# Attention over 64 heads: score buffers in one PSUM tile, and the order of all engines read from a table

## The chip, the cores and the metric

The kernel runs on one core of a Trainium2 chip. A core has five engines that run side by side, each with its own queue of instructions: TensorE (PE; its weight loads are shown as PEld) multiplies matrices into PSUM, VectorE (DVE) and ScalarE (ACT) work on PSUM and SBUF, GpSimd (POOL) on SBUF, and SyncE (SP) issues most DMA transfers. Instructions of different engines wait for each other by semaphores. The metric is the device time in microseconds of one execution. The median of three runs of the kernel before is 113.97 us (113.85 to 114.29).

## The reference

```python
batch, heads, seq, dim = 8, 8, 512, 64
...
scale = 1.0 / np.sqrt(q.shape[-1])
scores = np.einsum('bhqd,bhkd->bhqk', q, k) * scale
scores = scores - scores.max(axis=-1, keepdims=True)
attn = np.exp(scores)
attn = attn / attn.sum(axis=-1, keepdims=True)
return np.einsum('bhqk,bhkd->bhqd', attn, v).astype(np.float32)
```

There are 64 independent heads. Each has 512 x 512 scores; their exponentials, 16.8 million in all, weight the rows of v. Inputs and the output are float32, 8.4 MB each.

## The kernel before

**Tiling.** Heads are taken in 32 pairs; the two heads of a pair, called a and b here (h = 0, 1), share loads. A head's keys are cut into four blocks c of 128. One block of scores is 128 keys x 512 queries. Two blocks make a group, 1024 columns of 128 partitions, and a group is what one exponential works on. There are 128 groups; the last is done in two halves, so m runs from 0 to 128. In most pairs a group joins the same block of heads a and b, whose score matmuls use the two halves of TensorE's rows at the same time; in the first and the last pair a group joins two blocks of one head.

**The steps of a pair.** SyncE loads q, k and v of the pair, 256 KB each, into seven buffers per input. GpSimd casts each to float16 (`cast`, L515 for v, L525 for k and q). TensorE transposes k and q, four transposes each (`transposes`, L558), into one of two PSUM banks, and VectorE copies the result to SBUF (`copy`, L571). TensorE makes the scores of a group with two matmuls (`scores`, L598) in a PSUM buffer `st`, of which there are three. ScalarE writes the exponentials as float16 in `pt` (L602); 24 such buffers are there. Sixteen groups, listed in `ON_DVE`, go to VectorE instead: `raise_` (L625) makes the bits of a power of two from the scores, and five passes over SBUF (`pass_`: L642 and L651 take mantissa and exponent, L659, L661 and L665 a polynomial) correct it; the result is two tiles, `pe` and `pd`, so these blocks need two matmuls each where others need one.

**Values and output.** For 128 queries of a head, a unit, TensorE multiplies the four blocks' exponentials with v, to which a column of ones is joined (`values`, L704): 65 columns, the last being the sum of the weights. Seven units share a PSUM bank, one of the two that the transposes use too. VectorE takes reciprocals of the sums (`reciprocal`, L671) and multiplies (`normalise`, L676) into a ring of 112 units, from which SyncE stores heads, singly or in pairs. The last head has its own path (`last_values`, `finish`), with the last two groups' halves.

**The order.** All instructions are written out in the order that a planner, class `Plan`, finds: it steps through time in 5 ns with fixed costs for each instruction and decides for every engine what comes next. `ON_DVE`, due times of the casts and other numbers were set by hand in it. `cast_behind` ties each cast to an earlier instruction of VectorE (the number `behind` counts back along VectorE's instructions), so that GpSimd's casts lie beside chosen work of VectorE. A few exponentials (`KNOWN`) are tied to the cast six before.

**Buffers of scores.** `st` is a tile of a pool with three buffers, so a score pair waits until the reader of the group three before is done:

```python
st = ps_st.tile([P, 2, S], FP32, tag="st", name=f"st_{m}")
...
nc.tensor.matmul(st[:, x, cols], kc, qc[:, cols], start=True, stop=True)
```

**The start.** Pair 0 has its own code (`first_pair`): 52 small matmuls into a score buffer ahead of the data, casts split over three engines, and exponentials of its first group in two halves (L801).

Of the kernel before, what the change touches and what calls it, by code (L numbers as in the profile page):

```python
# [17 lines left out]
class Plan:  # L18

    SLOT, EXP, EXP_DONE, EXP_FIXED = 216, 853, 181, 64  # L20
    INTO, OUT_OF = 96, 96
    TRANSPOSE, V_UNIT = 222, 128
    TO_ACT, TO_DVE, TO_PE = 220, 210, 60

    COPY, NORM, RAISE = (601, 690), (50, 133), (1132, 1215)
    RECIPROCAL = 115
    SCALE, PRODUCT, EXTRA = 333, 600, 29
    COPY_1 = (400, 190)
    NORM_COLUMN, PASS_DONE = 67, 115
    PASSES = (SCALE, SCALE, PRODUCT, SCALE, PRODUCT)  # L30
    BITS = 2
    NEEDS = (None, None, 0, 2, 3)
    FIRST_EXP = 5000
    STEP = 5
    CALM, KEEN = 9000, 4
    FIRST_UNIT = 4
    KNOWN, OVER = (13, 15, 18, 20, 22, 24, 27, 42, 50, 61, 69, 97), 6
    ON_DVE = (5, 10, 16, 25, 28, 39, 44, 54, 63, 66, 74, 81, 91, 96, 103, 116)

    LATE_NORM, LATE_COPY, HURRY, SOON, BACKLOG = 700, 1500, 800, 160, 600  # L40
    LATE_MUL, WAIT = 400, 200
    SLACK, AHEAD = 0, 2

    CAST, CAST_PORT, CAST_DONE, TO_POOL = 557, 475, 130, 150
    SCALE_PORT, PRODUCT_PORT, GAP, REACH = 271, 537, 20, 5
    FIRST_LAND, LOAD, STORE, LATENCY, ISSUE = 5200, 752, 376, 2300, 470
    QUEUED, URGENT = 3500, 16
    PAIRED, STORE_ISSUE = 18, 520
    RAW, QK16, NV, NU = 7, 5, 12, 112
    PAIR, DUEK, DUEV, DUEL, PRE = 3300, 3550, 6000, 5000, 0  # L50

    def __init__(self, groups, pairs, first):
        self.groups, self.pairs = groups, pairs
        self.pe, self.act, self.dve = 7000, self.FIRST_EXP, 6300
        self.pool, self.port, self.dma = 4600, 4600, self.FIRST_LAND
        self.m, self.tiled = first, True
        self.read = []
        self.exps = {}
        for m in range(first):
            self.act += self.EXP + self.EXP_FIXED  # L60
            self.exps[m] = self.act + self.EXP_DONE
            self.read.append(self.exps[m])
        self.tq = {0: 5800}
        self.transposed = {0: 5800}
        self.next_t = 1
        self.part_t = 0
        self.banks = [5100, 5800]
        self.todo = [(g, h) for g in range(pairs) for h in range(2)]
        self.last = self.todo.pop()
        self.last_part = 0  # L70
        self.head = None
        self.units = self.FIRST_UNIT
        self.member = {b: m for m, grp in enumerate(groups) for b in grp}
        self.ready = []
        self.passes = []
        self.passed = {}
        self.raised = set()
        self.steps = []
        self.busy_dve = 0
        self.order, self.paired = [], 0  # L80

        late = {grp[0][0] for m, grp in enumerate(groups) if m in self.ON_DVE}
        due = []
        for g in range(pairs):
            scores = 5000 + self.PAIR * g
            if g:
                due += [(scores - self.DUEK, g, "k"), (scores - self.DUEK + 10, g, "q")]
            due.append((scores + self.DUEV + (self.DUEL if g in late else 0), g, "v"))
        self.due = sorted(due)
        self.uncast = list(self.due)  # L90
        self.casts = []
        self.landed, self.cast_done = {}, {}
        self.first_loads = [(g, n) for _, g, n in self.due if g < self.RAW]
        self.first_loads += [(self.RAW, "k"), (self.RAW, "q")]
        for x in self.first_loads:
            self.dma += self.LOAD
            self.landed[x] = self.dma
        self.loads, self.stores, self.stored = [], [], []
        self.sp = 1650 + 470 * len(self.first_loads)

    def note(self, t, *what):
        self.steps.append((t, len(self.steps)) + what)

    def trigger(self, t):

        ops = self.ops
        if not ops or ops[-1][1] <= t - 300:  # L110
            return 1, None
        n = len(ops) - 1
        while (
            n > 0
            and len(ops) - n < self.REACH
            and not ops[n][2]
            and ops[n][0] - ops[n - 1][1] <= self.GAP
        ):
            n -= 1
        if n > 0 and ops[n][0] - ops[n - 1][1] <= self.GAP:  # L120
            n -= 1
        return len(ops) - n, ops[n][1]

    def emit(self, t, back, after):
        _, g, n = self.uncast.pop(0)
        shared = (g, n) == (1, "q")
        self.note(t, "cast", g, n, back if t > self.CALM else 0)
        if not shared:
            self.casts.append((g, n, t if after is None else after + self.TO_POOL))
        if g + self.RAW < self.pairs:  # L130
            self.loads.append((g + self.RAW, n))

    def fits(self, t, soon=0):
        if not self.uncast:
            return False
        _, g, n = self.uncast[0]
        if n != "v" and g >= self.QK16 and self.transposed.get(g - self.QK16, 1e9) > t:
            return False
        return self.landed.get((g, n), 1e9) <= t + soon

    def step_pool(self, t):
        if self.uncast and self.uncast[0][1:] != (1, "q") and not self.casts and self.pool <= t:
            quiet = not self.passes and self.port <= t and not any(x[1] == "raise" for x in self.ready)
            if self.fits(t) and (quiet or self.uncast[0][0] - self.PRE < t):
                self.emit(t, 1, None)
        if self.casts and self.pool <= t and self.port <= t:
            g, n, after = self.casts[0]
            if after <= t and self.landed.get((g, n), 1e9) <= t:
                self.casts.pop(0)
                begin = max(self.pool, self.port, after, self.landed[(g, n)])  # L150
                self.pool = begin + self.CAST
                self.port = begin + self.CAST_PORT
                self.cast_done[(g, n)] = begin + self.CAST + self.CAST_DONE

    def step_sp(self, t):
        if self.sp > t or (self.loads and self.dma > t + self.QUEUED):
            return
        urgent = len(self.stores) > self.URGENT
        if self.loads and not urgent:
            g, n = self.loads[0]  # L160
            if self.cast_done.get((g - self.RAW, n), 1e9) <= t:
                self.loads.pop(0)
                self.note(t, "load", g, n)
                self.dma = max(self.dma, t + self.LATENCY - self.LOAD) + self.LOAD
                self.landed[(g, n)] = self.dma
                self.sp = t + self.ISSUE
                return
        if self.stores and self.stores[0] <= t:
            both = self.both()
            if both and (len(self.stores) < 2 or self.stores[1] > t):  # L170
                return
            heads = 2 if both else 1
            self.note(t, "store", heads)
            self.dma = max(self.dma, t + self.LATENCY - heads * self.STORE) + heads * self.STORE
            for _ in range(heads):
                self.stores.pop(0)
                self.stored.append(self.dma)
            self.paired += heads - 1
            self.sp = t + self.STORE_ISSUE

    def both(self):

        n = len(self.stored)
        g, h, u = self.order[n]
        return (
            self.paired < self.PAIRED
            and g < self.pairs - 2
            and h == 0
            and n + 1 < len(self.order)
            and self.order[n + 1][0] == g  # L190
            and u % self.NU + 8 <= self.NU
        )

    def room(self, t, u):
        heads = (u - self.NU - self.FIRST_UNIT + 3) // 4
        return heads <= 0 or len(self.stored) >= heads and self.stored[heads - 1] <= t

    def free(self, n=0):
        m = self.m + n
        if m >= len(self.groups):  # L200
            return 1e9
        g = self.groups[m][0][0]
        return max(0 if m < 3 else self.read[m - 3], self.tq.get(g, 1e9))

    def for_dve(self, m):
        return m in self.ON_DVE
# [692 lines left out]
```

## Time and profile before

| what | value |
|---|---|
| median of three runs | 113.97 us (113.85 to 114.29) |
| the profiled execution | 113.92 us |
| its span, first to last instruction | 112.1 us |
| mean granted TensorE clock | 0.994 |
| HBM read, written | 25.17 MB, 8.39 MB |
| exponentials on ScalarE (L602) | 110, 1144 ns mean |
| groups raised on VectorE (L625) | 16, 1216 ns mean |
| casts on GpSimd (L515, L525) | 93 of 128 x 512, 679 to 725 ns mean |

In the profile each row names a line of the kernel, an engine, an operation and its tiles, written as output <- input. On ScalarE and VectorE an instruction's time begins before its predecessor's has ended, so a mean duration is longer than the step from one instruction to the next; the step is what counts for a full engine. A timeline row with xN is N instructions of a line in a row. A row of waits says who waited for whom, with the total in us, the number of times and the longest.

### The profile page before, as it was taken

What the parts mean: (1) busy time and instruction counts of PE and PEld (TensorE: products, weight loads), DVE (VectorE), ACT (ScalarE), POOL (GpSimd) and SP (SyncE); (2) the same over time, 40 slices, a digit from 0 to 9 for tenths busy, and PEclk for the clock granted to TensorE, in tenths of its full rate; (3) what the DMA queues carried; (4) which work ended last, traced back from release to release, by engine and by line L of the source; (5) the groups of instructions that cost most, each with busy time, mean ns of one, the idle gap of its engine ahead of it and who ended that gap; (6) DMA issues with size and microseconds to landing.
All of it is one profiled execution on the core that took longest, in us unless ns stands there. A gap on an engine that the chain in (4) does not pass through costs nothing.

```text
span 112.1 us, 4408 instructions
## 1 busy us (share of the span) xinstructions
PE 103.2 (92%) x1728; PEld 69.4 (62%) x1728; DVE 100.8 (90%) x227; ACT 105.5 (94%) x118; POOL 65.9 (59%) x127
## 2 busy tenths in 40 slices
PE   7978889999799998999989999899999999999980
PEld 7634555766367766658647767577557577675660
DVE  1647999999999999999999999999999999997390
ACT  4599999999999999999999999999999999999970
POOL 2147768549756886495594786876784855600000
PEclk9999999999999999999999999999999999999997
DMA  3999999999999999999999999999999974142354
GB/s 106 276 359 353 345 350 347 355 336 349 345 347 336 341 346 343 354 364 375 370 358 382 350 355 377 354 372 362 343 366 305 349 245 143 52 141 99 97 167 161
DMA packets 35093, 33.84 MB, mean 302 GB/s; under 512 B 2304, under 2 KB 35072, under 8 KB 35072
## 3 DMA queue, kind: packets, MB, share of 16 engines
q1 hardware_dynamic: 34496, 33.04, 90.4%
q10 hardware_dynamic: 576, 0.52, 1.4%
q8 instruction: 13, 0.21, 0.8%
q14 instruction: 8, 0.07, 0.2%
HBM read 25.17 MB, written 8.39 MB: 299 GB/s over the span
## 4 chain that ended last, share of the span: by engine, by line
DVE 39%; PE 24%; DMA 15%; issue 8%; POOL 7%; SPq 3%; ACT 2%; POOLq 0%; ACTq 0%
PE o L704 13%; DMA v<-in_v_dram 10%; PE st L598 8%; DVE pd L625 8%; DVE tqk L571 7%; DVE ring L676 7%; DMA q<-in_q_dram 5%; DVE m L659 4%; POOL qkp L525 4%; DVE pd L665 4%; POOL vp L515 3%; PE tp L558 2%; SPq L509 2%; DVE m L642 2%; DVE pe L651 2%
## 5 line engine op out<-in xcount | busy, mean ns | idle before, releaser
L602 ACT ACTIVATE pt<-st 128x1024 f16<-128x1024 f32 (+1 forms) x110 | 100.3, 1144 | 0.2 <-PE st L598 0.2
L704 PEld LDWEIGHTS <-pt 128*128 128x128 f16 x880 | 38.8, 98 | 12.1 <-issue 10.2
L704 PE MATMUL o<-vp,pt 128*128 128x65 f16 x880 | 45.3, 194 | 0.4 <-POOL vp L515 0.2
L598 PE MATMUL st<-tqk 64*128 64x512 f16 (+1 forms) x250 | 41.7, 380 | 2.6 <-ACT pt L602 1.4
L525 POOL CAST qkp<-k 128x512 f16<-128x512 f32 x31 | 22.2, 717 | 11.3 <-DVE rc L671 5.3
L525 POOL CAST qkp<-q 128x512 f16<-128x512 f32 x30 | 21.7, 725 | 9.0 <-DVE rc L671 5.3
L515 POOL CAST vp<-v 128x512 f16<-128x512 f32 x32 | 21.4, 679 | 9.2 <-PE st L598 2.4
L676 DVE TENSOR_TENSOR ring<-o,rc 128x448 f32<-128x448 f32 (+2 forms) x37 | 22.3, 606 | 0.4
L704 PE MATMUL o<-vp,pe 128*128 128x65 f16 x128 | 21.8, 194 | 0.0
L704 PE MATMUL o<-vp,pd 128*128 128x65 f16 x128 | 21.7, 192 | 0.0
L558 PE MATMUL tp<-ident,qkp 128*128 128x128 f16 x248 | 19.6, 220 | 1.6 <-DVE tqk L571 0.8
L558 PEld LDWEIGHTS <-qkp 128*128 128x128 f16 x248 | 14.4, 97 | 9.9 <-issue 4.6
L571 DVE COPY tqk<-tp 128x1024 f16<-128x1024 f16 x30 | 20.3, 683 | 0.0
L625 DVE TENSOR_SCALAR pd<-st 128x1024 uint16<-128x1024 f32 x16 | 19.5, 1216 | 0.7 <-PE st L598 0.7
L598 PEld LDWEIGHTS <-tqk 64*128 64x128 f16 x250 | 10.7, 93 | 11.8 <-issue 4.6
L704 PEld LDWEIGHTS <-pe 128*128 128x128 f16 x128 | 12.5, 98 | 3.4 <-issue 3.3
L704 PEld LDWEIGHTS <-pd 128*128 128x128 f16 x128 | 12.5, 98 | 0.0
L659 DVE TENSOR_TENSOR m<-m 128x1024 f16<-128x1024 f16 x16 | 11.0, 685 | 0.0
L665 DVE TENSOR_TENSOR pd<-pd,m 128x1024 f16<-128x1024 f16 x16 | 10.9, 684 | 0.0
L671 DVE RECIPROCAL rc<-o 128x7 f32<-128x7 f32 (+2 forms) x37 | 7.4, 199 | 2.6 <-PE o L704 2.4
L661 DVE TENSOR_SCALAR m<-m 128x1024 f16<-128x1024 f16 x16 | 6.7, 418 | 0.1
L651 DVE TENSOR_SCALAR pe<-pd 128x1024 uint16<-128x1024 uint16 x16 | 6.6, 411 | 0.0
(51 smaller groups left out, 34.9 us busy)
## 6 DMA issues: line engine op xcount, KB each, us to landing
v<-in_v_dram SPq DMA_DIRECT2D x32, 256.0 KB, 5.8
k<-in_k_dram SPq DMA_DIRECT2D x31, 256.0 KB, 5.8
q<-in_q_dram SPq DMA_DIRECT2D x31, 256.0 KB, 5.9
out_dram<-ring SPq DMA_DIRECT2D x18, 256.0 KB, 5.5
out_dram<-ring SPq DMA_DIRECT2D x25, 128.0 KB, 2.2
k<-in_k_dram ACTq DMA_DIRECT2D x2, 128.0 KB, 2.8
q<-in_q_dram SPq DMA_DIRECT2D x2, 128.0 KB, 2.6
out_dram<-ring ACTq DMA_DIRECT2D x2, 128.0 KB, 1.9
```

The costliest lines, as they stand in the source:

```text
L515: return nc.gpsimd.tensor_copy(out=vps[g % NV][:, :, :, 0:D], in_=raw[g]["v"][:, :, :, :])
L525: return nc.gpsimd.tensor_copy(out=dst, in_=src[:, :, :, :])
L558: reads[g] = nc.tensor.transpose(tps[g][:, n, i, :], qkp[g][:, n, i, :], ident)
L571: nc.vector.tensor_copy(out=tqk[g][:, :, :], in_=tps.pop(g).rearrange("p n i c -> p n (i c)"))
L598: nc.tensor.matmul(st[:, x, cols], kc, qc[:, cols], start=True, stop=True)
L602: ins = nc.scalar.activation(out=pt[:, :, cols], in_=st[:, :, cols], func=EXP, scale=scale, bias=SHIFT)
L625: nc.vector.tensor_scalar(out=r["pd"][:, :, :], in0=r["st"][:, :, :], scalar1=BITS, scalar2=BIAS, op0=AluOp.mult, op1=AluOp.add,)
L651: ins = nc.vector.tensor_scalar(out=r["pe"][:, :, :], in0=u[:, :, :], scalar1=0x7C00, scalar2=None, op0=AluOp.bitwise_and,)
L659: ins = nc.vector.tensor_tensor(out=m16, in0=m16, in1=m16, op=AluOp.mult)
L665: ins = nc.vector.tensor_tensor(out=u16, in0=u16, in1=m16, op=AluOp.mult)
L676: nc.vector.tensor_tensor(out=ring[:, u % NU : u % NU + n, :], in0=o[:, x : x + n, 0:D], in1=rcs.pop(u)[:, 0:n].broadcast_to([P, n, D]), o ...
L704: nc.tensor.matmul(os[u // 7][:, u % 7, :], part[:, y * P : (y + 1) * P], vps[g % NV][:, h, c, :], start=(n == 0), stop=(n == len(parts) - 1),
```

## The change

- The three score buffers become three parts of one PSUM tile, `sts`. Group m uses part (m + 1) mod 3. Since the tile is now the same for all, the function `at` records who touches which part, and declares that TensorE and the other engines need not wait for each other over different parts, the copies of the first pair excepted.
- `Plan` is gone. A class `Order` holds the order of all engines as text: one letter for each step (S scores, T transposes, V a unit of values, C copy, N reciprocal, M product, R raise, K cast, G load, w and W stores of one and two heads, L and F the last head), and lists that say which head, cast, load or PSUM bank comes next. It is read, and the same functions are called. The numbers of steps of each kind are those of before. The table was found by a search outside the kernel, whose costs take ScalarE's rate from the ends of its instructions.
- The 16 groups of VectorE are at other places; pe and pd tiles are taken when the group is raised, not at its scores. `pt` has 21 buffers instead of 24.
- In the last pair the first two groups join both heads, as in other pairs.
- The text has room for groups split between the engines and for two groups in one exponential (`SPLIT`, `JOINED`, `WIDE`); these lists are empty.

```diff
+class Order:
+
+    ON_DVE = (5, 11, 16, 25, 28, 39, 45, 54, 62, 66, 75, 82, 91, 96, 108, 118)
+    SPLIT = ()
+    JOINED = ()
+    SINGLES, DOUBLES = 21, 1
+    PAIR_1 = "a0b0 a1b1 a2b2 a3b3"
+    LAST_PAIR = "a0b0 a1b1 a2a3 b2b3"
...
+    STEPS = (
+        "SKKTTKCSKSSRKTTSCVKVVaSNScVKSMVbTVdTKSCVKRSKTTSCSKeTTVgSKCSGKRVVGSKVGNSfSKMVGVhSTGkVTiVV"
...
+        "VVbVwScVwVVNSdVVeVVSMSVVwVVNVMVVVVSwNSMwVVVVwVVVwSNVMVVVLLwwNLMLFw"
+    )
+    HEADS = (
+        "0a 0b 1a 1b 3a 3b 2a 2b 5a 5b 4a 4b 6a 6b 8a 8b 7a 7b 10a 10b 9a 9b 12a 11a 11b 14a 12b "
...
+    CASTS = (
+        "1k 1q 2k 2q 0v 3k2 3q5 4k2 4q4 5k4 5q2 1v2 3v5 6k4 6q2 2v2 7k2 7q2 5v2 8k2 8q4 10k2 9q2 "
+        "4v2 9k2 10q3 6v4 11k3 13k2 11q2 12k3 8v4 12q2 7v3 13q2 14k3 15k2 10v3 14q2 15q5 9v2 16k2 "
...
+    LOADS = (
+        "8q 10k 8k 10q 9q 11k 9k 7v 11q 13k 12q 10v 14q 9v 13q 12k 14k 15q 8v 20k 16q 15k 16k 12v "
...
+            if step == "S":
+                yield "scores", m, m in self.ON_DVE
+                m += 1
...
-        if behind and latest:
-            tc.add_manual_dep(ins.ins, latest[behind - 1].ins.name, SYNC, reason="SBUF ports")
+        if behind:
+            tc.add_manual_dep(ins.ins, trail[-behind].ins.name, SYNC, reason="SBUF ports")
...
+    sts = ps_st.tile([P, 3, 2, S], FP32, tag="st", name="sts")
+    touched = []
+
+    def banks(m):
+        return sts[:, (m + 1) % 3], (m + 1) % 3
+
+    def at(ins, *where, tied=False):
+
+
+        pe = nc.tensor.engine
+        for other, there, also in touched[-64:]:
+            apart = there.isdisjoint(where) and not also
+            if apart and (other.engine == pe) != (ins.ins.engine == pe):
+                tc.declare_no_dep(ins.ins, other, reason="other banks")
+        touched.append((ins.ins, set(where), tied))
...
-        st = ps_st.tile([P, 2, S], FP32, tag="st", name=f"st_{m}")
+        st, bank = banks(m)
...
-            nc.tensor.matmul(st[:, x, cols], kc, qc[:, cols], start=True, stop=True)
...
+            at(nc.tensor.matmul(st[:, x, cols], kc, qc[:, cols], start=True, stop=True), bank)
...
+            at(ins, bank)
+            if half >= 0:
+                last.setdefault("exps", []).append(ins.ins)
...
     def last_values(part):
         if part == 0:
-            last["o"] = ps_st.tile([P, 2, S], FP32, tag="st", name="o_last")[
-                :, 0, 0 : NI * (D + 1)
-            ].rearrange("p (x d) -> p x d", x=NI)
+            st, _ = banks(len(groups))
+            last["o"] = st[:, 0, 0 : NI * (D + 1)].rearrange("p (x d) -> p x d", x=NI)
...
+                for halves in () if late else last["exps"]:
+                    tc.declare_no_dep(ins.ins, halves, reason="other banks")
```

More of the change, by code (lines that the diff above doesn't have):

```diff
@@ L579, in scores @@
         cols = slice(256 * half, 256 * half + 256) if half >= 0 else slice(0, S)
-        st = ps_st.tile([P, 2, S], FP32, tag="st", name=f"st_{m}")
+        st, bank = banks(m)
+        own = 0 if on_dve and m not in Order.SPLIT else 1 if on_dve else 2
+        first_of, second_of = m in Order.JOINED, m - 1 in Order.JOINED
         if on_dve:
-            tiles = {n: dpool.tile([P, 2, S], U16, tag=n, name=f"{n}_{m}") for n in ("pe", "pd")}
-            raised[m] = {"st": st, **tiles}
-            parts = [tiles[n].bitcast(FP16) for n in ("pe", "pd")]
+            raised[m] = {"st": st, "own": own, "bank": bank}
+        if own == 0:
+            pass
         elif half == 1:
             pt = last["pt"]
-        else:
-            pt = last["pt"] = ppool.tile([P, 2, S], FP16, tag="pt", name=f"pt_{m}")
+        elif first_of:
+            last["two"] = ppool.tile(
+                [P, 2, 2, S], FP16, tag="pt2", name=f"pt_{m}", bufs=Order.DOUBLES
+            )
+            pt = last["two"][:, int(bank == 2)]
+        elif second_of:
+            pt = last["two"][:, int(bank != 0)]
+        else:
+            pt = last["pt"] = ppool.tile(
+                [P, 2, S], FP16, tag="pt", name=f"pt_{m}", bufs=Order.SINGLES
+            )
         for x, (g, c, h) in enumerate(grp):
@@ L623, in raise_ @@
         r = raised[m]
-        dve(
-            nc.vector.tensor_scalar(
-                out=r["pd"][:, :, :],
-                in0=r["st"][:, :, :],
-                scalar1=BITS,
-                scalar2=BIAS,
-                op0=AluOp.mult,
-                op1=AluOp.add,
-            )
-        )
+        for n in ("pe", "pd"):
+            r[n] = dpool.tile([P, 2, S], U16, tag=n, name=f"{n}_{m}")
+        own = r["own"]
+        for x, b in enumerate(groups[m]):
+            if x >= own:
+                blocks[b] = [r[n].bitcast(FP16)[:, x, :] for n in ("pe", "pd")]
+        ins = nc.vector.tensor_scalar(
+            out=r["pd"][:, own:2, :],
+            in0=r["st"][:, own:2, :],
+            scalar1=BITS,
+            scalar2=BIAS,
+            op0=AluOp.mult,
+            op1=AluOp.add,
+        )
+        at(ins, r["bank"])
+        dve(ins)
     def pass_(m, s):
@@ L651, in pass_ @@
             ins = nc.vector.tensor_scalar(
-                out=r["pe"][:, :, :],
-                in0=u[:, :, :],
+                out=r["pe"][:, own:2, :],
+                in0=u[:, own:2, :],
                 scalar1=0x7C00,
@@ L749, in busy @@
     def busy(dst, n):
[L751 removed]
+        return nc.tensor.matmul(dst[:, 0:n], ones[:, 0:P], ones[:, 0:n], start=True, stop=True)
     def first_pair():
@@ L770, in first_pair @@
         nc.scalar.copy(k16[:, 1], tk[:, 1])
-        st0, pka, st1 = (
-            ps_st.tile([P, 2, S], FP32, tag="st", name=f"st_{n}") for n in ("0a", "ka", "1")
-        )
+        st0, pka, st1 = (sts[:, n] for n in range(3))
         pqa = ps_x.tile([P, 8, P], FP16, tag="x0", name="tp_qa")
@@ L820, in first_pair @@
         nc.vector.tensor_copy(out=qt[:, 1, 0:2], in_=pqb[:, 0:2])
-        pts = [ppool.tile([P, 2, S], FP16, tag="pt", name=f"pt_{m}") for m in range(3)]
+        pts = [ppool.tile([P, 2, S], FP16, tag="pt", name=f"pt_{m}", bufs=Order.SINGLES) for m in range(3)]
         for m in range(3):
@@ L835, in first_pair @@
         nc.vector.tensor_copy(out=qt[:, 1, 2:4], in_=pqb[:, 2:4])
-        st2 = ps_st.tile([P, 2, S], FP32, tag="st", name="st_2")
         for n in range(4):
-            busy(st2[:, 0], P)
-        first_scores(st2, 1, 0, 0, S, pts[2], 0, S)
+            at(busy(sts[:, 0, 0], P), 0)
+        first_scores(0, 1, 0, 0, S, pts[2], 0, S)
         first.update(kt=kt, qt=qt)
     with tc.manual_schedule():
-        plan = Plan(groups, NP, 3)
-        steps = plan.run()
+        order = Order()
         first_loads()
-        for g, name in plan.first_loads:
+        for g, name, _ in order.read(order.FIRST):
             load(g, name)
@@ L866 @@
         }
-        for what, *args in steps:
+        for what, *args in order.steps():
             do[what](*args)
```

540 lines of the change are left out of this document (124 added, 416 removed), and 9 rows, old and new, of tables (CASTS, HEADS, LOADS).

## The prediction

> **What bounds the kernel now.** First the page: the span and the busy time of each engine.
>
> ```profile
> span 112.1 us, 4408 instructions
> PE 103.2 (92%) x1728; PEld 69.4 (62%) x1728; DVE 100.8 (90%) x227; ACT 105.5 (94%) x118; POOL 65.9 (59%) x127
> ```
>
> The profiled execution took 113.92 us, so 1.8 us lie around its span; the median of the runs shown is 113.97 us, 0.05 above. The sum below is made against 113.92. Three engines are over 90% busy, so I ask which has no spare time. ScalarE's timeline (start, length), over the whole run then over the windows 26 to 30 and 26 to 46 us:
>
> ```profile
> 5.20 0.60 ACT L801 ACTIVATE pt<-st_0a 128x512 f16<-128x512 f32 x1 [0.43 <-PE st_0a L794]
> 5.69 0.59 ACT L801 ACTIVATE pt<-st_0b 128x512 f16<-128x512 f32 x1
> ...
> 7.98 1.06 ACT L602 ACTIVATE pt<-st 128x1024 f16<-128x1024 f32 x1
> 9.21 99.28 ACT L602 ACTIVATE pt<-st 128x1024 f16<-128x1024 f32 x109 [0.18 <-PE st L598]
> ...
> 25.60 4.86 ACT L602 ACTIVATE pt<-st 128x1024 f16<-128x1024 f32 x5
> ...
> 25.60 21.38 ACT L602 ACTIVATE pt<-st 128x1024 f16<-128x1024 f32 x23
> ```
>
> Exponentials overlap their neighbours, so I count from end to end. The two windows begin with the same one: 18 further ones take 21.38 - 4.86 = 16.52 us, 0.918 each. Halves, the first two rows, end 6.28 - 5.80 = 0.48 apart. The long row holds 109: one of 1.06 as the row above it, 106 whole ones and, at the end, two halves. (99.28 - 1.06 - 0.96) / 106 = 0.918 again, so the long stretch holds no idle time beyond the rounding, some 0.05 us. The only gap is at 9.21: shown as 0.18, by ends 10.27 - 9.04 - 0.92 = 0.31, call it 0.3. So some 0.35 us of idle ScalarE is all that any reordering can remove between the first exponential and the last.
>
> VectorE and TensorE by stage (length, then busy time and count of PE, PEld, DVE, ACT, POOL; clock; DMA):
>
> ```profile
> 60.00:70.00 10.00, 10.00 (x187) 6.85 (x183) 9.96 (x22) 10.00 (x12) 6.84 (x14) 1.00 1.09 365
> 90.00:100.00 10.00, 10.00 (x197) 7.08 (x198) 9.97 (x23) 10.00 (x12) 4.75 (x8) 1.00 0.46 151
> 100.00:109.00 9.00, 8.56 (x177) 6.06 (x177) 6.33 (x17) 8.49 (x11) 0.00 (x0) 1.00 0.32 104
> ```
>
> VectorE has hardly a gap before 100 us; its spare time, 2.7 us, lies in the last 9. A delay that VectorE takes early is therefore carried along until then. The tail:
>
> ```profile
> 108.01 0.84 PE L720 MATMUL o_last<-vp,pt 128*128 128x65 f16 x16
> 109.10 0.42 DVE L734 TENSOR_TENSOR obl<-o_last,rc_last 128x256 f32<-128x256 f32 x1
> 109.55 0.33 SPq L740 DMA_DIRECT2D out_dram<-obl  x1
> ```
>
> The last half exponential ends at 9.21 + 99.28 = 108.49; four matmuls, a reciprocal, a product and a store follow and end the span.
>
> **The change part by part.**
>
> *The number of exponentials: 0.* The new list of VectorE groups again has 16 members, so ScalarE still does 110 activations after the three of pair 0, at 0.918. No shorter start or tail is built: first loads, casts and first exponentials stay in their order. The floor is 113.92 - 0.35 = 113.6.
>
> *One PSUM tile: 0.* Group m uses part (m + 1) mod 3, three parts as before, and waits for the reader of m - 3 as now. The rows of this wait:
>
> ```profile
> PE st L598 <- ACT pt L602: 1.4, 5, 0.3
> PE st L598 <- DVE pd L625: 0.7, 2, 0.5
> ```
>
> 2.1 us in 7 waits, already hidden behind ScalarE's queue of ready scores. If the tile tied its parts together, each score pair would come after the exponential before it; that case is a rival. Above nothing there is one place: the late parts of the last head are not freed by name from the last half exponential. If part 2 waited for it, 4 more of the 16 matmuls above would follow 108.49: 4 x 0.03 = 0.12 us. I take 0, ends 0 and 0.12.
>
> *Fewer buffers of exponentials, 24 to 21: 0.* Counted along the new order, at most 19 are alive, as in the old one. The exponentials tied to the cast six back: six casts are at least 6 x 0.56 = 3.4 us old (rows below), 0.
>
> *TensorE's order.* The rows of a stretch (start, length):
>
> ```profile
> 36.84 0.29 PE L704 MATMUL o<-vp,pt 128*128 128x65 f16 x4
> 37.07 0.39 PE L598 MATMUL st<-tqk 64*128 64x512 f16 x2
> 37.39 0.43 PE L704 MATMUL o<-vp,pt 128*128 128x65 f16 x8
> 37.75 0.60 PE L598 MATMUL st<-tqk 64*128 64x512 f16 x4
> 38.29 0.62 PE L558 MATMUL tp<-ident,qkp 128*128 128x128 f16 x8
> ```
>
> From start to start a lone score pair takes 37.39 - 37.07 = 0.32 and two take 0.54: a further pair in a run adds 0.22, leaving the scores 0.10. One unit ahead of scores takes 0.23, two 0.36: a unit 0.13, entering the scores 0.10. The old order has 74 runs of scores and 147 such changes, the new one 87 and 173: 26 x 0.10 = 2.6 us more for TensorE, less 2 x 0.22 because two groups of the last pair now join both heads. Net 2.2 us. Its whole work by these steps is, before, 62 x 0.22 transposes + 252 x 0.13 units + 128 x 0.03 extra matmuls of VectorE groups + 129 x 0.22 score slots + 147 x 0.10 = 93 us of the 102 from 6.5 to 108.5. 9 us spare cover 2.2, so 0; where a run of units stands ahead of a lone pair the cover is only the scores held ready. Ends 0 and 0.2, taken 0.
>
> *VectorE's order, and casts against it.* VectorE's work is the same: 16 groups, the same passes, copies and products. New is which of its instructions each cast is released behind. VectorE's and GpSimd's timelines:
>
> ```profile
> 10.57 0.68 DVE L571 COPY tqk<-tp 128x1024 f16<-128x1024 f16 x1
> 10.72 0.62 POOL L525 CAST qkp<-k 128x512 f16<-128x512 f32 x1 [0.46 <-DVE pd L625]
> 11.42 0.40 DVE L642 TENSOR_SCALAR m<-pd 128x1024 uint16<-128x1024 uint16 x1
> 11.56 0.72 POOL L525 CAST qkp<-q 128x512 f16<-128x512 f32 x1 [0.23 <-DVE rc L671]
> 12.00 0.57 DVE L651 TENSOR_SCALAR pe<-pd 128x1024 uint16<-128x1024 uint16 x1
> 43.30 0.69 DVE L571 COPY tqk<-tp 128x1024 f16<-128x1024 f16 x1
> 43.90 0.62 DVE L676 TENSOR_TENSOR ring<-o,rc 128x448 f32<-128x448 f32 x1
> 44.43 0.68 DVE L665 TENSOR_TENSOR pd<-pd,m 128x1024 f16<-128x1024 f16 x1
> 44.58 1.01 POOL L525 CAST qkp<-k 128x512 f16<-128x512 f32 x1
> 45.63 0.42 DVE L642 TENSOR_SCALAR m<-pd 128x1024 uint16<-128x1024 uint16 x1
> 45.96 0.42 DVE L651 TENSOR_SCALAR pe<-pd 128x1024 uint16<-128x1024 uint16 x1
> 46.89 0.20 DVE L671 RECIPROCAL rc<-o 128x7 f32<-128x7 f32 x1
> 47.02 0.43 DVE L661 TENSOR_SCALAR m<-m 128x1024 f16<-128x1024 f16 x1
> 47.16 0.76 POOL L525 CAST qkp<-q 128x512 f16<-128x512 f32 x1 [1.57 <-DVE rc L671]
> 47.87 0.62 POOL L515 CAST vp<-v 128x512 f16<-128x512 f32 x1
> 48.46 0.60 POOL L525 CAST qkp<-k 128x512 f16<-128x512 f32 x1
> 49.02 0.61 POOL L525 CAST qkp<-q 128x512 f16<-128x512 f32 x1
> ```
>
> A cast alone takes 0.61, and casts in a row follow each other by 0.56. It starts 0.14 to 0.15 after the instruction that released it. If a pass over SBUF is then running, the cast waits: 1.01 behind L665, 0.76 behind L661. Where it is the other way, the pass waits: the cast at 11.56 was held 0.11 by L642, the pass at 12.00 took 0.57 instead of 0.42, so it really began at 12.15, 0.48 after the cast did at 11.67. Of the 89 casts released behind something, the old order has a pass next in 72, so GpSimd pays; the new one in 29, with a copy (0.60), product (0.53), reciprocal (0.13) or raise next in the others, so it can be VectorE that pays. Worked out at the tightest place near the start: the cast of q of pair 3 is now released five back, and follows k's at 10.72 + 0.56 = 11.28. Copy 2 ends at 11.17, pass 0 of group 5 runs 0.33 and holds the cast to some 11.44; a reciprocal, then pass 2 wants to begin at 11.63, and the cast holds it to 11.44 + 0.48 = 11.92: 0.3 us. Pass 2 and copy 3 behind it are late, and scores 12 wait for copy 3. The score buffers swallow part. I take half, 0.15, ends 0 and 0.3. After a copy or a product the pass comes 0.03 to 0.10 too early; ScalarE's ready buffer, one period of 0.92, covers each, 0.
>
> The Trainium skill ("SBUF — State Buffer", section on the two sides of SBUF) says the port pair that VectorE and GpSimd share is an exclusive lock, held for the whole instruction. The trace agrees that one waits for the other, but for 0.48 of a cast, not 0.61; by the whole cast the 0.3 would be 0.4.
>
> *Stores and loads on SP.* 73 loads and 45 stores as before. Loads now come in another order; the tightest is k of pair 31, issued with 26 stores ahead of it instead of 11, nine score steps before its transposes instead of 27. 126 steps in 102 us make 0.81 each, so it has 7.3 us. The landing row:
>
> ```profile
> k<-in_k_dram SPq DMA_DIRECT2D x31, 256.0 KB, 5.8
> SPq L694 <- DVE rc L671: 4.5, 3, 2.9
> ```
>
> 5.8 landing and 0.6 cast leave 0.9, and the last stretch moves 104 to 151 GB/s instead of 365, so it should land sooner: 0. It costs up to 2 us if SP stands 2.9 in front of a store, as the second row shows that it can.
>
> *The gaps that are there.* The 0.3 at 9.21 is set by loads and casts of pair 1, which stay: 0. The rounding's 0.05 may go: scores 7 now stand ahead of the first unit, which waits for a cast. Sum: 113.92 - 0.05 + 0.15 = 114.02, and 114.07 against the median. I give 114.1.
>
> **The rivals.**
>
> Slower, the mechanism: a cast wins a race that is open by 0.02 us. In the new order the cast of q of pair 10 is released at the end of the last pass of group 16 (call it 0). VectorE goes on with a reciprocal to 0.13, pass 0 of group 25 to 0.46, a product to 0.99, then pass 2. The cast starts at 0.15, is held as the one at 47.16 was, and the next cast, v of pair 6, follows 0.85 after that pass began (47.87 - 47.02), at 0.98. The pass wants to begin at 0.99. Cast first: the pass waits to 0.98 + 0.48, 0.47 late. Pass first: the cast waits 0.40 and nobody cares. Behind pass 2 stand copies 9 and 10, whose PSUM bank the units ahead of scores 36 need. The same stands at pass 2 of group 96, with the cast of q of pair 31. It decides where the cast is there first; each costs ScalarE 0.2 to 0.45. Time: 114.1 + 0.5 = 114.6. Against it: no near tie is in the trace. The Trainium skill's rule on that page is that whichever starts first gets the pair; by it the cast would win, the time 114.6, and 114.7 with the whole 0.61. Chance 0.28.
>
> Slower, second: the load of k of pair 31, or lags that VectorE carries along to the end: 115 to 116. Chance 0.08.
>
> The PSUM tile does not do what it says and the parts wait for each other: scores would take some 0.38 of each 0.92 period, 113 x 0.38 = 43 us, 157 us. Chance 0.02.
>
> Faster by over 0.5% (0.57 us, about what a measurement can tell from no change): needs more than the 0.35 that is idle, so a shorter start or tail that I do not see. 113.3. Chance 0.05.
>
> **How the numbers follow.** Forecast, no change that can be told, around 114.1: 0.57. Its own range is 113.6 (every gap gone) to 114.5 (0.3 + 0.12 + 0.05). Slower 0.28 + 0.08 + 0.02 = 0.38. The range takes in the lost race twice: 113.6 to 115.0.
>
> **What would show it.** Right: the exponentials again stand as one stretch of about 99.3 us, at 0.918; TensorE's busy time rises by some 2 us; passes longer than 0.43 (L642, L651, L661) or 0.69 (products) appear, adding to 1 to 2 us; casts of 1.01 become fewer. Wrong: idle time of ScalarE put to TensorE's scores, above all around scores 12, 36 and 109; or a first exponential or a tail that moved.

## The result, and the profile after

The changed kernel takes 140.48 us (median of 6 runs, 139.3 to 142.45); the kernel before took 114.06 us beside it. The ratio is 1.230, 95% interval 1.224 to 1.236. Medians and ranges take in every execution; the ratios leave out the few slow ones, over 1.5% above the fastest of their kernel. Forecast were 114.1 us and a range that ended at 115.0.

From the page of the changed kernel: the span, the busy time of each engine, the chain that ended last by engine, and three groups (line, engine, operation, tiles, count; busy time and mean ns of one; idle time of the engine just before them, and what ended most of it).

```profile
span 139.0 us, 4385 instructions
...
PE 112.3 (81%) x1728; PEld 74.3 (53%) x1728; DVE 104.4 (75%) x227; ACT 107.9 (78%) x118; POOL 62.6 (45%) x127
...
ACT 41%; PE 30%; DVE 19%; issue 7%; ACTq 0%; DVEq 0%
...
L331 ACT ACTIVATE pt<-sts 128x1024 f16<-128x1024 f32 (+1 forms) x110 | 102.7, 1030 | 24.2 <-DVE pd L362 22.0
L315 PE MATMUL sts<-tqk 64*128 64x512 f16 (+1 forms) x250 | 46.1, 393 | 18.8 <-DVE pd L362 12.4
...
L362 DVE TENSOR_SCALAR pd<-sts 128x1024 uint16<-128x1024 f32 x16 | 19.6, 1225 | 21.3 <-ACT pt L331 21.3
```

The work is that of before: 110 exponentials, 16 raises, 1728 matmuls. Idle time is new, and it stands in two rows that mirror each other: ScalarE's exponentials waited 22.0 us for VectorE's raises, and the raises 21.3 us for the exponentials. The chain passes from ScalarE to VectorE and back where one engine was full before. The waits of the same kernel (who waited for whom, total in us, times, longest) give the counts:

```profile
ACT pt L331 <- DVE pd L362: 22.0, 16, 1.7
DVE pd L362 <- ACT pt L331: 21.3, 15, 2.5
PE sts L315 <- DVE pd L362: 12.4, 13, 1.5
```

Sixteen waits of ScalarE for sixteen raises. The timeline around the first one, group 5:

```profile
8.31 2.85 ACT L331 ACTIVATE pt<-sts 128x1024 f16<-128x1024 f32 x3
...
8.74 1.03 PE L315 MATMUL sts<-tqk 64*128 64x512 f16 x6 [0.63 <-DVE tqk L255]
...
11.19 1.22 DVE L362 TENSOR_SCALAR pd<-sts 128x1024 uint16<-128x1024 f32 x1 [2.50 <-ACT pt L331]
...
12.51 3.85 ACT L331 ACTIVATE pt<-sts 128x1024 f16<-128x1024 f32 x4 [1.35 <-DVE pd L362]
```

The raise has its scores by 9.8 (8.74 + 1.03), and starts at 11.19, 0.03 after the third exponential ends at 11.16. Those three are the exponentials of groups 3, 4 and 6, which the order writes ahead of the raise; the last works on another part of the tile. The next exponential, of group 7, starts at 12.51, 0.10 after the raise ends at 12.41. So the two readers of the score tile run one after the other. An exponential takes 1.02 when alone, so the first one after the gap ends at 13.53: 2.37 after the one before it, where 0.92 is the step. 1.45 x 16 raises = 23.2 us. That is most of the 26.5 us by which the span exceeds the 112.5 us that the same order needs with three separate buffers (the second experiment). Of the 24.2 us of idle time before exponentials, a further 2.1 are waits for scores.

The cause can be read in the diff. A tile orders the instructions that touch it, in the order written. `at` declares two of them independent over different parts only if exactly one is TensorE's: `(other.engine == pe) != (ins.ins.engine == pe)`. A raise and an exponential are both not TensorE's, so that pair is never declared, though both only read. With three tiles the pair never met.

### The profile page after: what moved, and what is told of

Read it like the earlier page. It is cut to its first block, busy times and chain, and to the rows that moved or that the text cites. A ratio compares the mean times of both kernels' runs of the same rounds, so it can differ in the third digit from the quotient of the medians.

```text
span 139.0 us, 4385 instructions
## 1 busy us (share of the span) xinstructions
PE 112.3 (81%) x1728; PEld 74.3 (53%) x1728; DVE 104.4 (75%) x227; ACT 107.9 (78%) x118; POOL 62.6 (45%) x127
## 4 chain that ended last, share of the span: by engine, by line
ACT 41%; PE 30%; DVE 19%; issue 7%; ACTq 0%; DVEq 0%
ACT pt L331 39%; DVE pd L362 13%; PE o L445 12%; PE sts L315 11%; PE tp L248 4%; DVE tqk L261 3%; ACT pt L543 2%; PE sts L493 2%; DVE m L400 1%; DVE pd L406 0%; DVE ring L417 0%; DVE obl L476 0%; PE sts L460 0%; PE sts L535 0%; PE tp_qa L529 0%
## 5 line engine op out<-in xcount | busy, mean ns | idle before, releaser
L331 ACT ACTIVATE pt<-sts 128x1024 f16<-128x1024 f32 (+1 forms) x110 | 102.7, 1030 | 24.2 <-DVE pd L362 22.0
L315 PE MATMUL sts<-tqk 64*128 64x512 f16 (+1 forms) x250 | 46.1, 393 | 18.8 <-DVE pd L362 12.4
L445 PE MATMUL o<-vp,pt 128*128 128x65 f16 x880 | 50.6, 198 | 1.0 <-DVE tqk L261 0.7
L445 PEld LDWEIGHTS <-pt 128*128 128x128 f16 x880 | 41.4, 100 | 17.1 <-issue 14.5
L362 DVE TENSOR_SCALAR pd<-sts 128x1024 uint16<-128x1024 f32 x16 | 19.6, 1225 | 21.3 <-ACT pt L331 21.3
L215 POOL CAST qkp<-k 128x512 f16<-128x512 f32 x31 | 21.3, 686 | 23.2 <-DVE pd L362 6.2
L215 POOL CAST qkp<-q 128x512 f16<-128x512 f32 x30 | 19.4, 653 | 21.2 <-DVE rc L412 7.6
L315 PEld LDWEIGHTS <-tqk 64*128 64x128 f16 x250 | 12.4, 94 | 29.6 <-issue 20.2
L248 PE MATMUL tp<-ident,qkp 128*128 128x128 f16 x248 | 21.4, 225 | 2.4 <-DVE tqk L261 1.3
L445 PE MATMUL o<-vp,pd 128*128 128x65 f16 x128 | 22.6, 196 | 0.0
L400 DVE TENSOR_TENSOR m<-m 128x1024 f16<-128x1024 f16 x16 | 12.2, 761 | 0.0
```

The lines of the kernel that those rows point to most:

```text
L215: return nc.gpsimd.tensor_copy(out=dst, in_=src[:, :, :, :])
L248: reads[g] = nc.tensor.transpose(tps[g][:, n, i, :], qkp[g][:, n, i, :], ident)
L315: at(nc.tensor.matmul(st[:, x, cols], kc, qc[:, cols], start=True, stop=True), bank)
L331: ins = nc.scalar.activation(out=pt[:, 0:own, cols], in_=st[:, 0:own, cols], func=EXP, scale=scale, bias=SHIFT)
L362: ins = nc.vector.tensor_scalar(out=r["pd"][:, own:2, :], in0=r["st"][:, own:2, :], scalar1=BITS, scalar2=BIAS, op0=AluOp.mult, op1=AluOp.add,
L400: ins = nc.vector.tensor_tensor(out=m16, in0=m16, in1=m16, op=AluOp.mult)
```

## The experiments

All compute the whole result. "Before" beside them was 113.7 to 113.9 us.

**Readers freed.** The condition is widened to any two engines:

```diff
-            if apart and (other.engine == pe) != (ins.ins.engine == pe):
+            if apart and other.engine != ins.ins.engine:
```

> The kernel after, with one condition changed: any two engines, not only TensorE and another, are declared independent over different parts of the score tile. Theory 1 (readers of the one tile are kept in program order, so each raise on VectorE waits for the exponential written ahead of it and the next exponential waits for the raise): the 22.0 us of ScalarE waiting for pd and the 21.3 us of VectorE waiting for pt go to nearly 0, and the time falls to what was predicted for the order, 113.6 to 115.0, about 114.1. Theory 2 (the new order itself starves ScalarE, the tile is harmless): 135 to 141, ScalarE's idle time moves to TensorE's scores.

Measured: 115.15 us (114.89 to 116.2), ratio 1.012 (1.010 to 1.014), just above the range that was expected. Of the 26.4 us, 25.3 are gone with one condition, and no wait of ScalarE for a raise is left. Its exponentials after the first pair's wait only for scores:

```profile
ACT pt L331 <- PE sts L315: 0.8, 3, 0.3
```

**The order alone.** The new table of steps, with the score buffers as three tiles of a pool, as before:

```diff
-    sts = ps_st.tile([P, 3, 2, S], FP32, tag="st", name="sts")
...
-        return sts[:, (m + 1) % 3], (m + 1) % 3
+        return ps_st.tile([P, 2, S], FP32, tag="st", name=f"st_{m}"), (m + 1) % 3
```

> The order of the table with three separate score tiles from a pool, as in the kernel before; no declarations. Theory 1 (the tile ties readers): no ScalarE wait for pd, 113.6 to 115.0. Theory 2 (the order): 135 to 141. If it equals the run with freed readers within 0.5 us, the tile has no other cost.

> The table's order with three pool tiles once more, as the measure for the first kernel of this call: 114.3 and 0.5 per cent above before, as measured. Its distance to the first kernel is what the one tile costs with free readers.

Measured: 114.33 us (114.02 to 115.75), ratio 1.006 (1.004 to 1.008); a second time 114.46, ratio 1.006 (1.003 to 1.008). ScalarE's timeline of the first:

```profile
7.66 6.73 ACT L315 ACTIVATE pt<-st 128x1024 f16<-128x1024 f32 x7
14.56 19.38 ACT L315 ACTIVATE pt<-st 128x1024 f16<-128x1024 f32 x21 [0.17 <-PE st L309]
34.27 74.67 ACT L315 ACTIVATE pt<-st 128x1024 f16<-128x1024 f32 x82 [0.33 <-PE st L309]
```

There are two gaps, at scores 12 and at scores 36, the two places that the prediction had worked out. By ends, with 1.02 for a lone exponential: 14.56 + 1.02 - 14.39 - 0.92 = 0.27 and 34.27 + 1.02 - 33.94 - 0.92 = 0.43. The second one's race is in the timeline of all engines:

```profile
29.32 0.82 POOL L215 CAST qkp<-q 128x512 f16<-128x512 f32 x1 [0.60 <-DVE pd L390]
...
29.59 0.61 DVE L401 TENSOR_TENSOR ring<-o,rc 128x448 f32<-128x448 f32 x1
30.09 0.61 POOL L205 CAST vp<-v 128x512 f16<-128x512 f32 x1
30.13 1.11 DVE L384 TENSOR_TENSOR m<-m 128x1024 f16<-128x1024 f16 x1
...
31.16 1.27 DVE L261 COPY tqk<-tp 128x1024 f16<-128x1024 f16 x2
...
34.27 1.02 ACT L315 ACTIVATE pt<-st 128x1024 f16<-128x1024 f32 x1 [0.33 <-PE st L309]
```

The cast of v comes 0.04 us ahead of the pass. The pass takes 1.11 where the product passes of the prediction's rows took 0.68, so it lost 0.43; the two copies behind it are late, and so are the units and the scores. At the third place, group 96, ScalarE lost no more than 0.06. The second measurement's trace has the gap at scores 36 again, 0.45 by ends, and 0.23 at scores 12.

**The tile alone.** Before's planner and order, one tile, and the change's own `at`:

> The kernel before with its planner and its order, and only the score buffers in one tile with the change's declarations. Theory 1: 16 raises, each with a wait on both sides; ScalarE idle 16 x about 1.4 us = 22 us, so 134 to 142. Theory 2: 113.7 to 114.5.

Measured: 141.07 us (140.62 to 142.01), ratio 1.242 (1.237 to 1.246). Its waits:

```profile
DVE pd L643 <- ACT pt L618: 23.8, 16, 2.5
ACT pt L618 <- DVE pd L643: 20.2, 15, 1.4
PE sts L614 <- DVE pd L643: 16.8, 14, 1.8
```

The table is not needed for the loss: the tile does it under either order.

**Before's order, one tile, all readers freed.** The tile alone with the condition of the first experiment:

> The kernel before with its own order, the score buffers in one tile, and all engines, not TensorE and another alone, declared independent over different parts. If readers kept in program order are the whole cost of the tile: ScalarE's wait for pd falls from 20.2 us to under 1, and the time is within 0.3 of the kernel before. If the tile has a further cost of its own, as the 0.8 us between the two runs of the table's order hint: 114.3 to 114.9, with the first exponentials some 0.2 later because the copies of the first pair stay tied.

> Before's order in one tile with all readers freed and the tie at the start kept: 114.0, 0.3 above before, as measured; its distance to the second kernel is the tie.

Measured: 114.02 us (113.52 to 114.68), ratio 1.003 (1.001 to 1.005), and again 114.01, 1.003 (1.000 to 1.006). In ScalarE's timeline all 110 exponentials after the first pair's stand in one row:

```profile
8.35 100.15 ACT L618 ACTIVATE pt<-sts 128x1024 f16<-128x1024 f32 x110
```

A row of the timeline breaks only where the engine idles for more than 0.15 us, so its length has to be read too: a lone exponential, 107 steps of 0.918 and two halves of 0.48 make 100.2, so this row has no gaps at all. About half of the 0.3 us that is left of the medians is in the tail. The chain that ended last (start, length) has twice the matmuls behind the last exponential, before and then here:

```profile
108.55 0.31 PE o_last L720 x4
```

```profile
108.55 0.42 PE sts L738 x8
```

The span ends 3.6 us after the last exponential in before and in the order alone, and 3.8 after it in every kernel with one tile, 0.16 us later. That is the place in the last head which the prediction named and took at 0.

**One direction at a time.** In the changed kernel, the exponential need not wait for an earlier raise (first), or the raise not for an earlier exponential (second). The second is:

```diff
-            if apart and (other.engine == pe) != (ins.ins.engine == pe):
+            late = ins.ins.engine == nc.vector.engine and other.engine == nc.scalar.engine
+            if apart and (late or (other.engine == pe) != (ins.ins.engine == pe)):
```

> The kernel after with one direction freed: an exponential need not wait for a raise over other parts, the raise still waits for the exponential written ahead of it. If the two waits are one chain, half of it gone leaves: ScalarE's waits for pd (22.0 us) go to under 2, VectorE still waits for pt. A raise then begins up to one exponential late (0.9 to 2.5 us), which holds a score buffer and all of VectorE behind it: 118 to 132. If only ScalarE's own wait counts: 114 to 115.

> The kernel after with the other direction freed: a raise need not wait for the exponential written ahead of it, the exponential behind it still waits for the raise. Freeing the exponential alone gave 135.13 against 140.5. A raise can now begin as soon as its scores are there, so the exponential behind it finds it half done or done: ScalarE loses 0.3 to 1.2 us for each of 16 instead of 1.4, 118 to 133. If the two waits only work together: 114 to 116.

Measured, one run each: 135.13 and 118.16 us. The first missed what was expected. The second came out just inside its range, and not by the way that was expected: ScalarE waits for 5 raises, not for 16. The waits of the first, and under them one row of the second's:

```profile
DVE pd L363 <- ACT pt L332: 17.8, 14, 2.6
ACT pt L332 <- PE sts L316: 15.0, 26, 1.4
PE sts L316 <- DVE pd L363: 11.5, 11, 1.6
```

```profile
ACT pt L332 <- DVE pd L363: 3.0, 5, 0.9
```

Freeing ScalarE alone only moves its wait: 15.0 us for scores, which wait 11.5 us for the part that the late raise holds, which waits 17.8 us for an exponential. Freeing the raise alone lets it run as soon as its scores are there; 3.0 us of waits for it stay. So by these two runs the wait that makes the raise late carries some 22 of the 26 us, even where the idle time is booked on ScalarE.

**Casts released later.** On top of the order alone: v of pair 6 is released one instruction of VectorE back, not four (first); also q of pair 3 two back, not five, and q of pair 31 one back, not three (second):

```diff
-        "4v2 9k2 10q3 6v4 ...
+        "4v2 9k2 10q3 6v1 ...
```

> The order alone (three separate tiles), and one number of the table changed: the cast of v of pair 6 is released behind pass 2 of group 25 instead of behind the reciprocal three before it. In the run of the order alone that pass took 1.11 us instead of 0.68 and ScalarE lost 0.44 us by ends at scores 36. Theory A (the cast wins the shared port by some hundredths of a us, and the pass waits): the pass takes 0.68 again, the 0.44 is gone, the median falls from 114.33 by 0.3 to 0.45. Theory B (the units ahead of scores 36 are too many in any case): the gap stays, the median within 0.1 of 114.33.

> As before, and the casts of q of pairs 3 and 31 too are released later, so that none reaches the port just ahead of a product pass (pass 2 of groups 5, 25 and 96). Theory A: the gaps at scores 12 (0.28 by ends) and 36 (0.44) go, those late in the run shrink; 113.5 to 113.9, no slower than the kernel before. Theory B: 114.2 to 114.5.

Measured: 114.08 us (113.57 to 114.83), ratio 1.003 (1.001 to 1.006), and 114.29 (113.68 to 115.42), ratio 1.004 (1.002 to 1.007). ScalarE's timeline of each, the first over the long stretch, the second whole:

```profile
15.00 94.04 ACT L315 ACTIVATE pt<-st 128x1024 f16<-128x1024 f32 x103 [0.17 <-PE st L309]
```

```profile
7.98 100.49 ACT L315 ACTIVATE pt<-st 128x1024 f16<-128x1024 f32 x110
```

The first edit takes away the gap at scores 36, and the three edits together the one at scores 12 as well (by its length the one row still holds 0.3 us in gaps too small to break it); the profiled execution of the second ends its exponentials at 108.47, where before had 108.49. That shows each gap's cause. The medians are another matter: 0.25 us and 0.04 us below the 114.33 of the order alone, with intervals that overlap, and the second missed the 113.5 to 113.9 that was expected. The gain of the second over the first is not measured, and neither kernel is below before.

**What the tile still costs under the table's order.** Freed readers took 115.15, the order alone 114.33. One suspect was the start: the copies of pair 0 are kept tied to the first score matmuls. The tie of one of them, the second copy of k, was removed, under the table's order and under before's:

```diff
-        at(nc.vector.tensor_copy(out=kt[:, 0, 1], in_=pkc[:, 0]), 2, tied=True)
+        at(nc.vector.tensor_copy(out=kt[:, 0, 1], in_=pkc[:, 0]), 2)
```

> The changed kernel with its readers freed between all engines (as in the run on freed reads), and the second copy of k of pair 0 no longer tied to the first score matmuls, the only other thing that the one tile adds at the start. If that tie is what the one tile still costs once the readers are free, the first exponential starts some 0.2 us after the operands are there instead of 0.4, and the time falls from 115.15 to about 114.9 or below, towards the 114.33 of the order alone. If the tile costs something else (matmuls that wait for other parts, the last head), it stays within 0.2 of 115.15 and gaps of ScalarE stand where the order alone has none.

> Before's own order in one tile, with all readers freed, and the same tie of the first copy removed. If that tie is all the tile costs there, the time is that of before within 0.2 (the kernel with the tie was 0.3 above before); if not, it stays 0.3 above.

Measured: 115.29 us (115.18 to 117.55), ratio 1.012 (1.008 to 1.016), so the suspect falls: the first exponential comes sooner, after 0.40 us of idle time instead of 0.75, but the time does not fall (the ties of the other two copies stay). Under before's order it is 114.03, ratio 1.001 (0.998 to 1.003), which can't be told from the kernel with the tie. In its profiled execution the exponentials after the first pair's begin 0.6 us earlier than with the tie and end 0.2 later.

The other suspect was found in the trace: in the freed kernels nearly every raise has a second wait in front of it, a semaphore instruction on VectorE's queue, for the exponential that read the *same* part three groups earlier. It has long been done, and it says nothing new, since the scores have waited for it. It was removed by declaring any two readers independent, also over the same part (all three kernels below also lack the tie of the second copy of k):

```diff
-            if apart and other.engine != ins.ins.engine:
+            both = pe not in (other.engine, ins.ins.engine) and not also and not tied
+            if (apart or both) and other.engine != ins.ins.engine:
```

> The measure for the two above in the same call: readers of the same part still ordered. 115.2, as measured.

> The changed kernel in which two readers of the score tile are never ordered, over the same part neither: the matmul that fills a part still waits for the reader before it, so a reader need not. The raises then wait for TensorE alone, as with three pool tiles, and ScalarE's exponentials too. If the second wait of the raises is what is left of the tile's cost, the time is that of the order alone, 114.4 (0.5 to 0.6 per cent above before), and the raise near scores 82 starts without the 0.27 us of idle time. If something else in the one tile costs it, the time stays at 115.2.

> The same with the three casts released later (q of pair 3 two back, v of pair 6 one back, q of pair 31 one back). With three pool tiles those three edits gave 114.29 beside 114.33. Expected 114.2 to 114.4; if the late casts matter more once the raises are on time, down to 113.9.

Measured: 115.2 us with the second wait (114.82 to 115.28; ratio 1.010, 1.007 to 1.013), 114.95 without (114.58 to 115.02; 1.008, 1.005 to 1.011), and 114.42 without it and with the three later casts (114.02 to 115.07; 1.004, 1.001 to 1.007). First the view of the raise's line in the kernel with the wait: 15 semaphore instructions of 21 ns (without it, 1 is left). Then VectorE's timeline around scores 82, with the wait and without:

```profile
L362 DVEq EVENT_SEMAPHORE  x15: 21/21/21, 8.8 to 99.6; - x15
```

```profile
80.70 0.62 DVE L417 TENSOR_TENSOR ring<-o,rc 128x448 f32<-128x448 f32 x1
81.58 1.23 DVE L362 TENSOR_SCALAR pd<-sts 128x1024 uint16<-128x1024 f32 x1 [0.26 <-issue]
```

```profile
81.19 0.62 DVE L418 TENSOR_TENSOR ring<-o,rc 128x448 f32<-128x448 f32 x1
81.73 1.21 DVE L363 TENSOR_SCALAR pd<-sts 128x1024 uint16<-128x1024 f32 x1
```

With it the raise starts 0.88 after the product ahead of it, without it 0.54: 0.34 us, with nothing shown to have ended the 0.26. None of the other 15 raises is held by more than 0.1. The medians differ by 0.25 us, where 0.8 had been expected, and the intervals of the ratios overlap, so the gain is not shown by them. The traces show it in the 82 exponentials from scores 36 on, which took 74.67 us in the order alone. With the wait, without it, and the last row of the kernel with the three later casts:

```profile
34.13 75.12 ACT L331 ACTIVATE pt<-sts 128x1024 f16<-128x1024 f32 x82 [0.34 <-PE sts L315]
```

```profile
34.52 74.88 ACT L332 ACTIVATE pt<-sts 128x1024 f16<-128x1024 f32 x82 [0.34 <-PE sts L316]
```

```profile
37.55 71.11 ACT L332 ACTIVATE pt<-sts 128x1024 f16<-128x1024 f32 x78 [0.16 <-ACT pt L332]
```

Of the 0.45 us above the order alone, 0.24 is gone with the wait. What stays is one new gap, which the last row shows: an exponential held until the one ahead of it on ScalarE has ended, 0.27 us by ends, and 0.25 at the same exponential of the kernel without the later casts. The order alone doesn't have it; what orders the two isn't shown. With the tail's 0.16 that places some 0.4 of the 0.5 to 0.6 us by which 114.95 lies above the order alone (114.46 and 114.33), and by the ratios (1.008 and 1.006) the two can't be told apart. The kernel mended in both ways is level with the order alone, and slower than before by 0.4%. No version tried is faster than before.

## Why the prediction was wrong

**The step that failed is "One PSUM tile: 0".** It followed the three parts and the wait of a matmul for "the reader of m - 3", that is, writer against reader, and held that these waits stay as they are. They do. It did not ask which pairs of engines `at` leaves ordered: ScalarE's exponentials and VectorE's raises, two readers that had never shared a tile. That pair is worth 25.3 us under the table's order (140.48 against 115.15) and 27.1 under before's (141.07 against 114.02). The rows of before would have priced it. A raise takes 1.22; between two exponentials that may not run beside it, it delays the second by itself and the steps around it, 1.45 as measured, 16 times. The prediction's sign of being wrong was idle time put to TensorE's scores; 22.0 of the 24.2 us was put to the raises.

**The rival named for the tile** had the right object, parts that wait for each other, and the wrong pair. It was priced as scores behind the exponential, 43 us and 157 us, which the declarations in the diff exclude; it stood at 0.02 and outside the range. The rival that happened needed no failure of the change: what it declares is what it does, and the readers are simply not in it.

**The order's own steps held in the main**, with the first rival's lost race, and can be judged in the run with the order alone.
- *The floor.* ScalarE full at 0.918 us per exponential: with three later casts, and with before's order in one tile and its readers freed, the 110 stand in one row. No version's median came under before.
- *Casts against VectorE, place 1.* Ends 0 and 0.3, 0.15 taken; 0.27 measured at scores 12, so the score buffers swallowed hardly any of it.
- *The late parts of the last head.* Ends 0 and 0.12, 0 taken; 8 matmuls follow the last exponential instead of 4, and the tail is 0.16 longer.
- *The race open by 0.02.* The rival at scores 36 happened as worked out: the cast first by 0.04, the pass 0.43 late against 0.47, ScalarE 0.43 late against 0.2 to 0.45. It did not repeat at group 96. The rule that the prediction drew from the Trainium skill ("SBUF — State Buffer", section on the two sides of SBUF), that whichever starts first gets the pair, agrees with this trace; holding for the whole instruction does not: the pass lost 0.43, so it began 0.47 after the cast did, while the cast's row is 0.61 long.
- *The sum.* With 0.6% above before, 113.97 x 1.006 = 114.6: the order alone came out at that rival, not at the 114.1 of the forecast, and within the range. The upper end of the forecast's own range, 114.5, is not the sum of its terms: 113.97 with the ends 0.3, 0.12 and TensorE's 0.2 is 114.6.
- *TensorE's changes: 0.* Said to add some 2 us of busy time and to be covered. In the order alone:

```profile
PE 104.5 (93%) x1728; PEld 70.4 (63%) x1728; DVE 102.3 (91%) x227; ACT 105.9 (94%) x118; POOL 63.4 (56%) x127
```

  1.3 us more than the 103.2 of before, and VectorE 1.5 more, within the 1 to 2 us named for longer passes. With the three later casts no gap of ScalarE above 0.17 us is left that TensorE's own changes could have made.
- *Fewer buffers, loads on SP: 0.* Neither shows in a gap of ScalarE in these runs.

## What to carry to other kernels

When several buffers become parts of one tile, list every pair of engines that touches it, readers against readers too, and check each pair against what the change declares independent; a pair that is left out runs strictly in the written order. Price such a pair by the reader that the full engine has to wait for, times its count, as the least it costs (here 16 raises of 1.22 make 19.5 of some 25 us), and look for the wait that makes a reader late, not for the engine on which the idle time is booked. A dependency that is always met can still have a price where it puts a second wait in front of an instruction on a full engine: here 0.34 us at one raise of 16 under the table's order, and no gap in the first trace under before's, where 14 raises had such a wait.

## What was not expected of the hardware

The granted clock fell in the stalled kernel. The window from 10 to 30 us (length; busy time and count of PE, PEld, DVE, ACT, POOL; clock; DMA share; GB/s), after and then before:

```profile
10.00:30.00 20.00, 16.18 (x201) 10.32 (x200) 15.17 (x29) 14.83 (x17) 8.27 (x15) 0.83 1.09 348
```

```profile
10.00:30.00 20.00, 18.34 (x277) 11.53 (x274) 19.86 (x40) 20.00 (x23) 14.21 (x27) 1.00 1.09 347
```

TensorE did less and was granted 0.83 instead of 1.00. That is a mean: the clock was at half in three stretches of some 3.4 us and at 1.00 between them. Two of the three:

```profile
23.60:26.90 3.30, 3.18 (x41) 2.59 (x41) 2.44 (x5) 3.30 (x4) 1.05 (x3) 0.50 1.09 348
64.60:67.80 3.20, 3.20 (x46) 2.20 (x42) 2.89 (x7) 2.52 (x3) 1.55 (x3) 0.50 1.08 362
```

The whole-run means are 0.963 after, 0.951 with the tile alone and 0.962 with the exponential freed, against 0.994 before and 1.000 with the raise freed. What sets it was not tried. The gaps counted above are those of raises and exponentials, on two other engines. Of ScalarE's 2.1 us of waits for scores, 1.6 end in or just behind these two stretches, at 27.36, 28.74, 66.74 and 68.01; whether the clock made them, or anything else in the rest of the loss, stays open.
